# A hybrid decoder step: sampled tokens' PSUM tiles move into attention's five banks, and the filler projections get a second bank

## The chip, the cores and the metric

The kernel runs on one core of a Trainium2 chip. The metric is the device time of one execution in microseconds (us), as the median of several runs; less is better. Beside it stands a profile, which is one execution recorded instruction by instruction on the core's engines: PE (matrix products and transposes, written to PSUM), PEld (its weight loads), DVE (the vector engine), ACT (the activation engine), POOL and SP (which here mostly start transfers). PSUM has eight banks for all of them; each holds 128 x 512 float32 values.

## What is computed

One layer of a decoder for 1024 prompt tokens and 8 sampled tokens that share the weights. The prompt's and the samples' rows go through the same input projection, then two branches: sparse attention over the best 256 keys of each query, and a gated delta rule with a recurrent state. Both are gated, merged, and followed by a SwiGLU block.

```
xn = rms_norm(x, norm_mix)
h = xn @ w_in
q, k, v, iq, ik, iw, u, a, b, z, gl = jnp.split(h, pts, axis=-1)
...
o_a = attend(q, k, v, iq, ik, iw).reshape(B, T, BRANCH_WIDTH)
...
o_b, s_new = gated_delta_chunked(qb, kb, vb, g, beta, s0)
o_b = rms_norm(o_b.astype(x.dtype), delta_norm) * jax.nn.silu(z.reshape(B, T, H_B, DV_B))
...
proj = jnp.einsum('btnc,ncd->btnd', jnp.stack([o_a, o_b], axis=2), w_branch)
gates = jax.nn.sigmoid(gl.reshape(B, T, 2, D_MODEL))
x = x + jnp.sum(gates * proj, axis=2) @ w_out
x = x + (jax.nn.silu(gg) * uu) @ w_down
```

For the 8 sampled tokens, attend reads a paged cache of 1024 past keys (gathered by a page table) plus the token's own key, and the delta rule is one step on a given state of 8 x 4 matrices of 128 x 128.

## The kernel before

Float32 values are split into two parts (split, lines 185 to 188: ACT writes the high part, DVE subtracts to get the low part), and a product is made of three passes over them (mm3, lines 163 to 165). A projection of 128 output columns over all 1,032 tokens is done in three chunks of 344 tokens; each chunk fills one PSUM tile pj with 24 passes (12 for the merge), and is then emptied by ACT or DVE.

The stages that matter here come in this order in the program. `scan` runs the delta rule over eight chunks of the prompt, and projections of q, k, v and of gates (gate, L863 empties their tile into gs) between them. `attention` then does the following:

- For the eight blocks of 128 queries, from the longest (1,024 keys) to the shortest (128 keys), and two key groups each, `att_scores` makes the scores of four heads (L267 transposes the queries, L1024 and L1025 are the score products, L1026 on DVE adds the mask and takes the extreme of the row, L1031 on ACT takes the exponential, L1037 the reciprocal, L1039 on ACT and L1041 on DVE scale), and `att_out` transposes the weights (L1056), splits them (L187 into ph, L188 into pl) and multiplies with the values (L1060, L1061 into PV; L1066 and L1067 empty it). The scores of one group are woven with the output of the group ahead of it.
- The seven gates that are left (gate_steps) are woven with `sample_delta`, the delta step of the sampled tokens: L1458 to L1495 prepare it, L1482 multiplies the state, and eight times a mask (L1517, DVE, one buffer), a product (L1521, PE) and four updates (L1524, DVE) renew four matrices of the state, which are loaded and stored by SP (L1436, L1525).
- The first 21 chunks of `merge_b` (products of o with w_branch, emptied by L878) are woven with `sample_attend`, the attention of the sampled tokens: gathers of the cache by POOL (L1246), transposes (L1346), splits into kTp, products (L1358), a softmax, transposes of its weights (L1389) and products with the values (L1406).

The written order is only the input to a scheduler. It gives every engine one fixed queue of instructions, drawn from all stages whose buffers it has, and an engine then works through its queue in that order. Tiles of one tag in a pool share a ring of buffers (bufs) that is handed out in the order in which the program asks; a tile waits until the earlier holder of its buffer is done.

In `attention` eight banks are shared out like this: pj has one bank (the filler projections), tq has one (all tiles of sample_delta and sample_attend, through ptq), PT has five and PV has one (through pT and pv). `sample_attend` keeps its tiles in memory (the pools mergeg and sample) that the pool of `sample_delta` and the projections' input xhi, xlo give back.

Of the kernel before, what the change touches and what calls it, by code (L numbers as in the profile page):

```python
# [33 lines left out]
def weave(a, n, b=iter(()), m=0):  # L34

    x = 0
    for j, _ in enumerate(a):
        while x < m and x * n <= j * m:
            next(b, None)
            x += 1  # L40
    for _ in b:
        pass
# [12 lines left out]
class K:  # L55
# [849 lines left out]
    def attention(self, end_x):  # L905
        nc, I = self.nc, self.I
        ps, end_ps = self.pool("fillers", space=PSUM)
        self.pq = self.pf = ps
        self.pj_bufs = 1
        self.ps, end_pa = self.pool("att", space=PSUM)  # L910
        self.ap, end_a = self.pool("att")
        self.sd, end_sd = self.pool("sampled")
        last, last_n = iter(()), 0
        for i in ATT:
            for g in range(2):
                P = [None] * 4
                weave(self.att_scores(i, g, P), 13, last, last_n)
                last, last_n = self.att_out(i, g, P), i + 2
        weave(last, last_n)
        gates = list(self.gates)  # L920
        weave(self.gate_steps(gates), 5 * len(gates), self.sample_delta(), 13)
        end_x()
        end_sd()
        mg, end_mg = self.pool("mergeg")
        self.wk, self.end_sa = self.pool("sample", side="right")
        mp, end_m = self.pool("mergeb", side="right")
        steps = self.merge_b(self.load_split(mp, self.d_ob), mg)
        self.sample = self.sample_attend(mg)
        weave(islice(self.sample, 33), 25, islice(steps, BESIDE), BESIDE)
        end_pa()  # L930
        end_ps()
        self.pj_bufs, self.tp_bufs = 5, 2
        self.open_psum("ps5")
        self.pf, self.end_pf = self.pool("psm", space=PSUM)
        self.stage = self.sp.tile([128, 2048], F32, name="rs", tag="kvb", bufs=1)
        x0 = self.sp.tile([128, 4224], F32, name="x20", tag="S", bufs=1)
        self.x2h = [x0[:, 0:4 * T].rearrange("p (j t) -> p j t", j=4)]
        self.x_T(0)
        self.pq = self.ps
        for _ in steps:  # L940
            pass
        end_m()
        end_mg()
        end_a()
# [917 lines left out]
```

## Time and profile before

| | us |
|---|---|
| median of 3 runs (lowest to highest) | 1775.06 (1770.65 to 1778.87) |
| the profiled execution | 1773.84 |
| its span, first to last instruction | 1771.8 |
| PE busy | 1721.3 (97%) |
| PEld busy | 1662.9 (94%) |
| DVE busy | 1214.9 (69%) |
| ACT busy | 847.1 (48%) |
| POOL busy | 30.4 (2%) |

Busy time counts each moment once, however many instructions of an engine overlap in it. The mean duration in a group of instructions is longer than the step from one to the next where instructions are pipelined, so such durations must not simply be added on PE or DVE. The chain of work that ended last is 85% PE.

### The profile page before, as it was taken

Reading aid. Unit: us, or ns where it says so; the run is one execution under the profiler, and the core shown is the slowest. Engines: PE = TensorE matmul, PEld = TensorE weight load, DVE = VectorE, ACT = ScalarE, POOL = GpSimd, SP = SyncE. Lnnn points to the kernel's source line nnn. Section 1 sums busy time; section 2 is a strip of 40 time slices with the busy share of each in tenths; the row PEclk is TensorE's granted clock in tenths of the full one; section 3 lists DMA queues with packets and bytes.
Section 4 is the critical chain, followed back from the end, with each engine's and each line's share of the span. In section 5 each row is a group of like instructions: output and inputs, shape, how many; then the busy total and the mean of one; then the engine's idle time right before and its main releaser. Section 6 shows DMA issues by size and latency. Waiting matters only on the chain.

```text
span 1771.8 us, 31786 instructions
## 1 busy us (share of the span) xinstructions
PE 1721.3 (97%) x12300; PEld 1662.9 (94%) x12300; DVE 1214.9 (69%) x2809; ACT 847.1 (48%) x1575; POOL 30.4 (2%) x61
## 2 busy tenths in 40 slices
PE   6999999999999999999899999999999999999998
PEld 5998989999999989979898999999999999999998
DVE  7676658999799868799856488776666665733322
ACT  5566467777835436687534254443333333412112
POOL 0001100000000000000000000000000000000000
PEclk9999999999999999999999999999999999999999
DMA  6015434433645543354667444332222223722122
GB/s 209 30 38 159 127 101 137 147 97 114 175 127 160 174 144 95 111 166 144 220 203 237 141 128 138 102 108 85 72 85 84 79 78 128 236 68 81 45 81 69
DMA packets 293595, 218.02 MB, mean 123 GB/s; under 512 B 39292, under 2 KB 267456, under 8 KB 292412
## 3 DMA queue, kind: packets, MB, share of 16 engines
q1 hardware_dynamic: 291716, 205.50, 38.2%
q0 software_dynamic: 1728, 10.49, 1.7%
q8 instruction: 97, 1.59, 0.4%
q14 instruction: 54, 0.44, 0.1%
HBM read 154.17 MB, written 61.87 MB: 122 GB/s over the span
## 4 chain that ended last, share of the span: by engine, by line
PE 85%; DMA 6%; DVE 4%; ACT 3%; issue 2%; SPq 0%; POOL 0%; ACTq 0%; DVEq 0%; POOLq 0%
PE pj L163 15%; PE pj L165 15%; PE pj L164 15%; PE F L1734 2%; PE F L1736 2%; PE F L1735 2%; PE A L1734 2%; PE A L1735 2%; PE A L1736 2%; PE D L1734 2%; PE D L1736 2%; PE D L1735 2%; PE PT L1056 2%; PE B L1735 1%; PE B L1734 1%
## 5 line engine op out<-in xcount | busy, mean ns | idle before, releaser
L163 PE MATMUL pj<-xhi,whi 128*128 128x344 f32 x912 | 297.9, 327 | 5.2 <-ACT gs L863 4.3
L165 PE MATMUL pj<-xhi,wlo 128*128 128x344 f32 x912 | 293.7, 322 | 0.0
L164 PE MATMUL pj<-xlo,whi 128*128 128x344 f32 x912 | 292.9, 321 | 0.0
L187 ACT ACTIVATE whi<-wraw 128x1024 fp32r<-128x1024 f32 (+4 forms) x126 | 115.2, 914 | 245.4 <-PE pj L164 197.5
L163 PEld LDWEIGHTS pj<-xhi,whi 128*128 128x128 f32 x912 | 171.8, 188 | 9.5 <-ACT gs L863 5.6
L164 PEld LDWEIGHTS pj<-xlo,whi 128*128 128x128 f32 x912 | 171.7, 188 | 2.5 <-issue 1.1
L165 PEld LDWEIGHTS pj<-xhi,wlo 128*128 128x128 f32 x912 | 171.7, 188 | 1.2
L164 PE MATMUL pj<-act,whi 128*128 128x344 f32 x528 | 170.2, 322 | 0.0
L163 PE MATMUL pj<-act,whi 128*128 128x344 f32 x528 | 169.9, 322 | 0.0
L165 PE MATMUL pj<-act,wlo 128*128 128x344 f32 x528 | 168.8, 320 | 0.7 <-DVE wlo L188 0.7
L188 DVE TENSOR_TENSOR wlo<-wraw,whi 128x1024 fp32r<-128x1024 f32 (+3 forms) x104 | 116.4, 1119 | 48.2 <-ACT whi L187 47.3
L1798 DVE TENSOR_TENSOR x<-pj,x 128x344 f32<-128x344 f32 x96 | 48.7, 514 | 142.4 <-PE pj L165 142.4
L769 DVE TENSOR_SCALAR_CACHE_REDUCE kvb<-S,cand 128x384 bf16<-128x384 f32 (+3 forms) x128 | 103.7, 810 | 2.0
L165 PEld LDWEIGHTS pj<-act,wlo 128*128 128x128 f32 x528 | 99.3, 188 | 1.0 <-DVE wlo L188 1.0
L163 PEld LDWEIGHTS pj<-act,whi 128*128 128x128 f32 x528 | 99.3, 188 | 0.6
L164 PEld LDWEIGHTS pj<-act,whi 128*128 128x128 f32 x528 | 99.3, 188 | 0.0
L1735 PE MATMUL A<-hb,wlo 128*128 128x258 f32 x328 | 92.6, 283 | 0.0
L1734 PE MATMUL A<-hb,wlo 128*128 128x258 f32 x328 | 92.5, 282 | 0.0
L1736 PE MATMUL A<-hb,wlo 128*128 128x258 f32 x328 | 92.3, 282 | 0.0
L1734 PE MATMUL D<-hb,wx 128*128 128x258 f32 x308 | 87.1, 283 | 0.0
L1735 PE MATMUL D<-hb,wx 128*128 128x258 f32 x308 | 87.0, 282 | 0.0
L1736 PE MATMUL D<-hb,wx 128*128 128x258 f32 x308 | 87.0, 283 | 0.0
(604 smaller groups left out, 4785.8 us busy)
## 6 DMA issues: line engine op xcount, KB each, us to landing
wraw<-in_w_gate_up SPq DMA_DIRECT2D x50, 512.0 KB
wraw<-in_w_in SPq DMA_DIRECT2D x38, 512.0 KB
d_act<-x SPq DMA_DIRECT2D x41, 258.0 KB
araw<-d_act SPq DMA_DIRECT2D x20, 516.0 KB
d_g<-gs SPq DMA_DIRECT2D x48, 172.0 KB
wraw<-in_w_out SPq DMA_DIRECT2D x16, 512.0 KB
wraw<-in_w_branch SPq DMA_DIRECT2D x12, 512.0 KB
wraw<-in_w_down SPq DMA_DIRECT2D x16, 384.0 KB
```

The source lines that it names most:

```text
L163: nc.tensor.matmul(ps, lh, rh, start=(j == 0), stop=False)
L164: nc.tensor.matmul(ps, lh, rl, start=False, stop=False)
L165: nc.tensor.matmul(ps, ll, rh, start=False, stop=(j == last))
L187: self.nc.scalar.activation(hi, src, AF.Copy)
L188: self.nc.vector.tensor_tensor(lo, src, hi.bitcast(F32), op=ALU.subtract)
L769: nc.vector.tensor_scalar(junk[:r, :n], s, thr[:r, j:j + 1], 0.0, op0=ALU.is_lt, op1=ALU.add, accum_out=cnt[:r, j:j + 1])
L1056: nc.tensor.transpose(p[:, j, :], P[j][:, 128 * s:128 * s + 128], self.ident)
L1734: nc.tensor.matmul(p, lh, rh, start=(first and k == 0), stop=False, skip_group_check=True)
L1735: nc.tensor.matmul(p, lh, rl, start=False, stop=False, skip_group_check=True)
L1736: nc.tensor.matmul(p, ll, rh, start=False, stop=(k == 3), skip_group_check=True)
L1798: nc.vector.tensor_tensor(xv, p, xv, op=ALU.add)
```

## The change

The pool of the fillers gives both its banks to pj. The tiles of the sampled tokens (ptq) are for the time of `attention` taken from the ring PT, by setting ptq to pT; after the stage the original ptq is used again. All else is as written before, and nothing is added to or taken from the arithmetic. Line numbers after line 909 are one greater, and after line 932 two greater (L1521 becomes L1523).

```diff
--- before.py
+++ after.py
@@ -905,8 +905,9 @@
     def attention(self, end_x):
         nc, I = self.nc, self.I
         ps, end_ps = self.pool("fillers", space=PSUM)
-        self.pq = self.pf = ps
-        self.pj_bufs = 1
+        self.pf = ps
+        self.pj_bufs = 2
+        self.ptq = self.pT
         self.ps, end_pa = self.pool("att", space=PSUM)
         self.ap, end_a = self.pool("att")
         self.sd, end_sd = self.pool("sampled")
@@ -929,6 +930,7 @@
         weave(islice(self.sample, 33), 25, islice(steps, BESIDE), BESIDE)
         end_pa()
         end_ps()
+        del self.ptq
         self.pj_bufs, self.tp_bufs = 5, 2
         self.open_psum("ps5")
         self.pf, self.end_pf = self.pool("psm", space=PSUM)
```

The scheduler's queues change from the end of the scan on. Names in the rows below: pj is a projection's tile, PT a tile of the ring of five, tq the sampled tokens' tile before, PV attention's output; P are attention's weights, ph and pl their split parts; k2, q2 and v2 are keys, queries and values; sum, sk4, S0, st and skq belong to the sampled tokens' delta step; xhi, xlo, whi and wlo are a projection's operands.

On PE, in the middle of attention (the second largest block of queries), the queue before:

```order
L1060 MATMUL PV_7330<-ph_7357,v2_6586 128x512
L165 MATMUL pj_9237<-xhi_114,wlo_9205 128x344
L1061 MATMUL PV_7330<-pl_7358,v2_6586 128x512
L1024 MATMUL PT_7402<-k2_6585,q2_7311 128x448
L1025 MATMUL PT_7402<-k2_6585,q2_7311 128x448
L1521 MATMUL tq_9414<-sum_9412,sk4_9004 128x512
L1056 MATMUL PT_7407<-ident_84,P_7172 128x128
```

And the same place now:

```order
L1026 MATMUL PT_7398<-k2_6585,q2_7311 128x448
L1027 MATMUL PT_7398<-k2_6585,q2_7311 128x448
L1063 MATMUL PV_7330<-pl_7358,v2_6586 128x512
L1062 MATMUL PV_7330<-ph_7378,v2_6586 128x512
L1026 MATMUL PT_7402<-k2_6585,q2_7311 128x448
L1027 MATMUL PT_7402<-k2_6585,q2_7311 128x448
L1058 MATMUL PT_7407<-ident_84,P_7172 128x128
```

The projection pass (L165) and the sampled product (L1521) have left this place, and attention's own passes follow one another.

On PE, where the sampled tokens' delta step begins, the queue before, ahead of attention's first scores:

```order
L1458 MATMUL tq_8741<-ssq3_8643,ones_1543 128x96
L1459 MATMUL tq_8741<-sgd_8649,ones_1543 128x64
L267 MATMUL PT_6958<-ident_84,qn_6955 128x128 x2
L1482 MATMUL tq_8858<-skq_8640,st_8637 128x2 x8
L163 MATMUL pj_8972<-xhi_114,whi_8967 128x344
L164 MATMUL pj_8972<-xlo_115,whi_8967 128x344
L165 MATMUL pj_8972<-xhi_114,wlo_8968 128x344
```

And the place where it runs now, at the last two products of attention (L1062, L1063):

```order
L1062 MATMUL PV_8587<-ph_8593,v2_6586 128x512
L1484 MATMUL PT_8858<-skq_8640,st_8637 128x2 x2
L1063 MATMUL PV_8587<-pl_8594,v2_6586 128x512
L1484 MATMUL PT_8858<-skq_8640,st_8637 128x2 x4
L1484 MATMUL PT_8858<-skq_8640,S0_8891 128x2 x4
L1484 MATMUL PT_8858<-skq_8640,S0_8897 128x2 x4
L1495 MATMUL PT_9000<-sC_8744,ones_1543 128x32
L1496 MATMUL PT_9000<-ident_84,skr_8763 32x128
L1497 MATMUL PT_9000<-ident_84,skS_8764 32x128
L1523 MATMUL PT_9092<-sum_9034,sk4_9004 128x512
L1523 MATMUL PT_9192<-sum_9100,sk4_9004 128x512
```

The state products (L1482, now L1484) moved from attention's beginning to its end, and the eight products of L1523 stand in a row behind them, where projections stood between them before.

On DVE, the updates of the state before, among attention's splits (pl) and scores (L1026, ISA):

```order
L1517 TENSOR_TENSOR sum_9100<-sv4_9005,eye4_9006 128x512
L188 TENSOR_TENSOR wlo_9205<-wraw_9203,whi_9204 128x1024
L1026 ISA P_7172,st_7171<-PT_7173,msk_1966 128x448
L1026 ISA st_7171 128x1
L188 TENSOR_TENSOR pl_7152<-PT_7146,ph_7151 128x512
L1026 ISA P_7193,st_7171<-PT_7194,msk_1966 128x448
L1026 ISA st_7171 128x1
L188 TENSOR_TENSOR pl_7188<-PT_7182,ph_7187 128x512
L1026 ISA P_7172,st_7171<-PT_7177,msk_1966,st_7171 128x448
L1026 ISA st_7171 128x1
L1524 SCALAR_TENSOR_TENSOR st_8637<-st_8637,sC_8744,tq_9192 128x128 x4
L1517 TENSOR_TENSOR sum_9201<-sv4_9005,eye4_9006 128x512
```

And now, behind all of attention's work:

```order
L1526 SCALAR_TENSOR_TENSOR S0_9199<-S0_9199,sC_8744,PT_9293 128x128 x4
L1519 TENSOR_TENSOR sum_9302<-sv4_9005,eye4_9006 128x512
L1526 SCALAR_TENSOR_TENSOR S0_9300<-S0_9300,sC_8744,PT_9366 128x128 x4
L1519 TENSOR_TENSOR sum_9374<-sv4_9005,eye4_9006 128x512
L1526 SCALAR_TENSOR_TENSOR st_8637<-st_8637,sC_8744,PT_9404 128x128 x4
L1519 TENSOR_TENSOR sum_9412<-sv4_9005,eye4_9006 128x512
L1526 SCALAR_TENSOR_TENSOR st_8637<-st_8637,sC_8744,PT_9414 128x128 x4
L1519 TENSOR_TENSOR sum_9423<-sv4_9005,eye4_9006 128x512
L1526 SCALAR_TENSOR_TENSOR S0_9421<-S0_9421,sC_8744,PT_9425 128x128 x4
L1519 TENSOR_TENSOR sum_9434<-sv4_9005,eye4_9006 128x512
L1526 SCALAR_TENSOR_TENSOR S0_9432<-S0_9432,sC_8744,PT_9436 128x128 x4
```

The masks and updates alternate with nothing between them. Each mask uses the one buffer of the mask before.

## Rows read from the trace of the kernel before

**Rows 1.** the stretches table: busy us (x instructions) of PE, weight loads, DVE, ACT, POOL; granted clock, DMA share, GB/s:
```profile
580.00:646.00 66.00, 62.95 (x466) 58.93 (x465) 47.35 (x161) 24.39 (x58) 0.00 (x0) 1.00 0.50 145
646.00:872.00 226.00, 222.78 (x1425) 201.34 (x1426) 198.94 (x528) 161.02 (x335) 8.66 (x10) 1.00 0.46 145
872.00:912.00 40.00, 35.52 (x252) 30.75 (x251) 19.05 (x40) 9.68 (x20) 0.95 (x1) 0.91 0.53 183
```

**Rows 2.** the timeline of PE, first and last of 45 projection passes (start us, duration us):
```profile
870.32 0.32 PE L163 MATMUL pj<-o,whi 128*128 128x344 f32 x1
...
877.26 0.32 PE L165 MATMUL pj<-o,wlo 128*128 128x344 f32 x1
```

**Rows 3.** groups by line of PE, 646 to 872 us (busy us, mean ns, idle before):
```profile
L163 PE MATMUL pj<-xhi,whi 128*128 128x344 f32 x96 | 31.5, 328 | 0.0
...
L163 PE MATMUL pj<-o,whi 128*128 128x344 f32 x84 | 27.9, 332 | 0.0
...
L1521 PE MATMUL tq<-sum,sk 128*128 128x512 f32 x8 | 3.2, 394 | 0.0
```

**Rows 4.** the timeline of PE, sampled tokens' passes between attention's:
```profile
646.74 1.95 PE L1482 MATMUL tq<-skq,st 128*128 128x2 f32 x16
...
785.11 0.60 PE L1346 MATMUL tq<-ident,kvg 128*128 128x128 f32 x4
...
869.13 1.12 PE L1358 MATMUL tq<-kTp,q2S 128*128 128x256 f32 x8
```

**Rows 5.** groups by line of PE, 580 to 646 us:
```profile
L163 PE MATMUL pj<-xhi,whi 128*128 128x344 f32 x72 | 24.2, 336 | 2.4 <-ACT gs L863 2.4
```

**Rows 6.** groups by line of DVE, 646 to 872 us:
```profile
L188 DVE TENSOR_TENSOR pl<-PT,ph 128x512 fp32r<-128x512 f32 x72 | 48.9, 685 | 6.8 <-ACT ph L187 4.8 <-PE PV L1061 1.6
L1026 DVE CUSTOM_DVE_ANT_0 P<-PT,msk 128x512 f32<-128x512 f32 (+5 forms) x64 | 33.5, 534 | 3.2 <-PE PT L1025 2.8
L1026 DVE CUSTOM_DVE_ANT_0 P<-PT,msk,st 128x512 f32<-128x512 f32 (+3 forms) x32 | 20.6, 645 | 1.5 <-PE PT L1025 0.7
L1041 DVE TENSOR_SCALAR P<-P,st 128x1024 f32<-128x1024 f32 (+7 forms) x32 | 16.4, 517 | 0.5
L270 DVE TENSOR_TENSOR q<-PT,q 64x256 fp32r<-64x256 f32 x32 | 13.5, 422 | 2.5 <-ACT q L269 1.5
L1067 DVE TENSOR_TENSOR oT<-PV,pvt 64x512 f32<-64x512 f32 x16 | 11.0, 686 | 0.6 <-ACT pvt L1066 0.3
...
L1026 DVE DVE_READ_ACCUMULATOR2_ANT st<- 128x1 f32 x96 | 7.9, 82 | 0.0
...
L1517 DVE TENSOR_TENSOR sum<-sv,eye 128x512 fp32r<-128x512 f32 x8 | 5.5, 684 | 0.0
L1037 DVE RECIPROCAL st<-st 128x2 f32<-128x2 f32 x32 | 4.9, 157 | 1.0 <-ACT P L1031 0.8
```

**Rows 7.** the timeline of DVE, back to back:
```profile
684.41 0.61 DVE L1026 CUSTOM_DVE_ANT_0 P<-PT,msk 128x448 f32<-128x448 f32 x1
...
684.95 0.68 DVE L188 TENSOR_TENSOR pl<-PT,ph 128x512 fp32r<-128x512 f32 x1
685.55 0.67 DVE L1026 CUSTOM_DVE_ANT_0 P<-PT,msk,st 128x448 f32<-128x448 f32 x1
...
686.57 1.12 DVE L1524 SCALAR_TENSOR_TENSOR st<-st,sC,tq 128x128 f32<-128x128 f32 x4 [0.34 <-PE tq L1521]
```

**Rows 8.** groups by line of ACT, 646 to 872 us:
```profile
L1031 ACT ACTIVATE P<-P,st 128x1024 f32<-128x1024 f32 (+7 forms) x64 | 49.3, 771 | 18.1 <-DVE st L1026 17.8
L187 ACT ACTIVATE ph<-PT 128x512 fp32r<-128x512 f32 x72 | 41.8, 591 | 14.5 <-PE PT L1056 9.2 <-PE PV L1060 3.6 <-ACT gs L863 0.6
L1039 ACT ACTIVATE P<-P,st 128x1024 f32<-128x1024 f32 (+7 forms) x32 | 24.6, 772 | 1.8 <-DVE st L1037 1.6
```

**Rows 9.** the stretches table, around a fall of the granted clock:
```profile
880.00:885.00 5.00, 2.29 (x16) 1.46 (x15) 3.01 (x8) 0.58 (x2) 0.00 (x0) 0.86 0.78 270
885.00:890.00 5.00, 4.58 (x16) 4.58 (x17) 2.50 (x6) 1.79 (x4) 0.00 (x0) 0.50 0.68 188
```

## The prediction

> **What bounds the kernel now.** I read the stretches first, then the engines inside one of them. The change only acts between the end of the delta scan and the end of the sampled tokens' attention, so I cut that time in three [rows 1]: the scan's tail (580 to 646 us), prompt attention (646 to 872) and the sampled tail (872 to 912). In all three the tensor engine (PE) is the full engine: it is idle 66 - 62.95 = 3.05 us, 226 - 222.78 = 3.2 us and 40 - 35.52 = 4.5 us. VectorE (DVE) is busy 198.94 of the 226 us and ScalarE (ACT) 161.02. The reader should see how little can be won here: the PE idle time of all three stretches is 10.8 us, and that is the ceiling of any gain from shorter waits on PSUM. Everywhere else the program is not touched.
>
> Why is PE full during attention? Because four kinds of work are mixed there: attention's own matmuls, gate projections, merge projections, and the sampled tokens' products. A projection pass costs 0.158 us start to start: 44 steps from 870.32 to 877.26 [rows 2]. In the attention stretch 96 x 3 passes are gates and 84 x 3 are merges [rows 3], so 540 x 0.158 = 85 us are projections. The sampled products in it are 64 passes of L1482 at 1.95/16 = 0.12, 64 transposes at 0.60/4 = 0.15 and 64 products at 1.12/8 = 0.14 [rows 4], 26 us, less the drain of the last pass in each row; I take 22 us, and 4 us for the small ones. What is left of 222.8 us is attention itself: 222.8 - 85 - 26 = **112 us** of PE.
>
> **The change, part by part.** *A second bank for projections.* The wait that it takes away is on one row: L163 idle 2.4 us in the scan's tail behind ACT's evacuation gs [rows 5]. In the attention stretch the same row shows no idle time at all [rows 3], since PE had other work to run while ACT emptied the bank. So the direct gain is 2.4 us, and at most the 3.05 us above. The second bank has another effect: the scheduler can run gate projections back to back, and puts them earlier. Counted in the two orders, 2,448 passes on x stand on PE ahead of attention's first transposition before, and 2,633 now. These 185 passes x 0.158 = 29 us fall in the scan's tail, where PE has 3 us to spare, so attention starts about 26 us later, near 672 us. This by itself is no loss, as the same passes are then missing later: inside attention only 103 passes on x remain (288 before), and none of the merge's (240 before).
>
> *Sampled tiles in attention's banks.* These tiles are requested after all of attention's in the program, and a shared ring of five banks is handed out in that order. So sampled work that ran beside attention in its own bank (the eight products of L1521 stand among attention's rows before) now stands behind it: all eight products follow the last attention matmul on PE, and their 32 updates (L1524) and eight masks (L1517) stand in one block on DVE, with nothing in between. The merge's work follows as well, because its tiles lie in memory that the sampled state must leave first. SP's loads of the state and its stores move along with it. POOL's order is the same; its key gathers (L1246) now find free memory earlier, and cost nothing on the path.
>
> *What attention costs alone.* PE has 112 us of attention and 103 x 0.158 = 16 us of projections, together 128 us. DVE's attention work, by its rows [rows 6] 48.9 + 33.5 + 20.6 + 16.4 + 13.5 + 11.0 + 7.9 + 4.9 = 156.7 us, is a sum of durations that overlap: back to back a score of 448 columns, 0.61, and the reading of its minimum, 0.08, take 0.54 from start to start, and a split of 0.68 takes 0.60 (684.41 to 684.95 to 685.55) [rows 7]. At these steps the 156.7 us shrink to about 131 us. ACT's three largest groups alone are 49.3 + 41.8 + 24.6 = 116 us [rows 8]. So three engines have some 130 us each, and every tile passes through all three in turn, with two heads' groups in flight. Bounds for the stretch: 131 us if DVE never waits; 185 us if DVE is 70% full. I take **163 us**. About 17 us of it are the start, where 77 of the 103 passes stand between the first scores and DVE has only some 8 us of work; the other 131 - 8 = 123 us I take at 0.84 full (146 us). The nearest row is DVE's 198.94/226 = 0.88 [rows 1], and that was reached with much independent sampled work at hand, which is gone now, and the last heads are short and wait on each other. PE is then idle 163 - 128 = 35 us, from 672 to 835 us.
>
> *What the sampled tail costs alone.* Each of the eight state updates is a closed circle of one buffer: mask 0.68, product 0.39, four updates 1.12, and hand-overs of about 0.06 each [rows 3, 6, 7], some 2.25 us, so 18 us for eight, with 0.4 us of PE in each. Ahead of them stand the small vector operations and products of the state, some 4.5 us more. PE has about 8 us to do in these 22.5 us: 15 us idle. Then the attention of the sampled tokens begins with loads into memory that the state has just left (store, load, first transposes: some 5 us idle), and its eight halves run through ACT, DVE and PE in turn with only 24 projection passes between them (4 us idle); 3 us I keep for the softmax. Together **27 us**, with bounds of 15 (the state update half hidden behind the last heads) and 40 (every load late). After that merge projections fill PE as before.
>
> *Sum.* 35 + 27 = 62 us of new idle time, less the 10.8 us that PE idles there now, is 51 us. The profiled execution took 1773.84 us, so 1825 us. The median of the three runs, 1775.06, is 1.2 us above it, within their own spread (1770.65 to 1778.87), so I state **1825 us** against the median. About 0.5% (9 us) is what a measurement of this kernel can tell from no change.
>
> **The rivals.**
>
> *Tight packing, a smaller loss.* Attention runs near its floor (145 us, 17 us idle) and the state update overlaps the last heads (18 us): 17 + 18 - 11 = 24, so 1798 us. For it speaks that DVE fills 0.88 of the stretch while fighting for PE; against it that no covering work is left.
>
> *The clock falls.* After a stretch in which PE was busy 2.29 of 5 us, the granted clock was 0.50 (the 1.2 GHz level) for the next 5 us [rows 9]. If PE's gaps in attention and in the sampled tail bring the lower level for a quarter of the 163 us, PE's work there grows by a quarter of 128, 32 us; DVE's slack hides perhaps half, so I add 16 us there, 9 us in the tail and 5 us in the first merge passes: 30 us more, 1855 us. Against it: at 62.95 of 66 us the clock stayed 1.00, and the gaps may be short. The Trainium skill, TensorE: Matmul & The Clock Gate, section "A second HAM failure mode: psum-queue depth-cycling", describes such a case: cycling through PSUM banks leaves small gaps between groups of matmuls, and the clock swings. No run here shows it yet.
>
> *Faster: the banks were the limit.* The place is the five-bank ring. Sampled tiles were tied to one bank, and with five each transposition can run ahead of its split. If DVE holds attention to its floor of 131 us (3 us idle) and the sampled tail idles under 8 us because later projections can be drawn forward, then 3 + 2 - 11 = -6 to -8, some 1767 us. It decides at 10.8 us of new idle time in all: below that the change wins. Against it stand the orders: no projection is left to draw on in most of attention, and none stands between the eight state updates. The Trainium skill, Perfetto Trace Analysis, "Identifying Performance Opportunities", says that the same gap repeating on an engine that should be saturated can mean too little PSUM. Such gaps are scarce here, 3.2 us in 226 [rows 1], so by this trace the rule promises little.
>
> *Nothing happens.* The order on PE moves, but the moved work only changes places and PE stays full: 1775 us. It would need fillers in attention, which the order does not have.
>
> **How the numbers follow.** The forecast (roughly 1810 to 1845) gets 0.60, tight packing 0.17, the clock 0.14, faster 0.05, nothing 0.04. The low end takes in tight packing (1798); the high end takes DVE at 0.73 (57 us idle), the tail at its bound of 40, less 11: 86 us, some 1860, which also covers the clock case. So 1797 to 1862 us leaves out the last two cases and the tips of the others. Slower by over 0.5% has 0.60 + 0.17 + 0.14 = 0.91, within 0.5% 0.04, faster 0.05.
>
> **What would show it.** In the profile after, attention's first score should stand near 672 to 678 us and the last head end near 835; in between PE should be busy only about four fifths, with DVE above it, and L1056's successor and the score matmuls waiting for DVE and ACT. Behind it a stretch of some 25 us with PE mostly idle and the eight state updates on DVE in a row. The gs wait of L163 should be near zero. The sampled output products (L1406 before) should come some 50 us later. I am wrong if PE stays above 95% in attention, if the state updates' waits are filled by projections, or if the granted clock is at the lower level over tens of microseconds. Then the time is that of the rival named.

## The result, and the profile after

The changed kernel takes 1853.91 us (1853.48 to 1854.12, three runs) against 1775.06 us before: a ratio of 1.0441, 95% interval 1.0415 to 1.0466. It is slower, inside the range on record (1797 to 1862), 29 us above the forecast of 1825. The profiled execution has a span of 1852.2 us, 80.4 us more than before.

All of it lies between the end of the scan and the first half of the projection to w_out: the first product of the norm behind that half (L1632, now L1634) stands at 1101.3 us and stood at 1019.5, 81.8 us earlier. So the four stretches up to there hold the answer: the scan's tail, attention (first score to last product with the values), the sampled tokens' tail (to their last transposition, L1412, now L1414), and the merge with that first half of w_out. Stretches table of the changed kernel: length, then busy us (x instructions) of PE, weight loads, DVE, ACT, POOL, then granted clock, DMA share, GB/s:

```profile
580.00:678.00 98.00, 98.00 (x708) 95.44 (x707) 57.67 (x176) 34.52 (x78) 0.00 (x0) 1.00 0.48 142
678.00:843.00 165.00, 148.48 (x777) 115.69 (x775) 143.05 (x394) 132.71 (x283) 4.33 (x5) 0.93 0.19 59
843.00:976.00 133.00, 105.56 (x652) 89.84 (x652) 62.98 (x147) 25.33 (x46) 5.66 (x6) 0.81 0.55 174
976.00:1101.00 125.00, 114.25 (x822) 111.42 (x823) 71.60 (x137) 46.99 (x85) 0.00 (x0) 0.97 0.64 204
```

Against [rows 1]: PE, idle for 3.2 us of 226 in attention's old stretch, is now idle for 16.5 of 165, and for 27.4 of 133 behind it. In attention PE (148.48), DVE (143.05) and ACT (132.71) are all near the 165 us and none is full: they wait for each other. The clock column is new too: 0.93, 0.81, 0.97 where nearly all of it was 1.00.

Where each new microsecond of PE lies can be added up. In slices of about 4 us I took PE's idle time, its busy time x (1 - granted clock), and the rest, its busy time x granted clock. The middle one counts what the lower clock (1.2 in place of 2.4 GHz) cost PE if all its work then takes twice as long. A projection pass took 1.8 times as long there (0.287 us a step from 884.46 to 887.33 us, 0.158 in [rows 2]), so that column is rather too high and the last rather too low:

| 580 us to L1632, now L1634 | length | idle | lower clock | rest |
|---|---|---|---|---|
| before | 439.5 | 13.6 | 2.8 | 423.1 |
| after | 521.3 | 54.7 | 25.4 | 441.2 |
| difference | 81.8 | 41.1 | 22.6 | 18.1 |

The last two columns grow by 40.7 us, and the page of the profile has the same from its other end: PE's busy time, 1721.3 us before, is 40.1 us longer, though the work is the same. Its busy row and the shares of the chain that ended last:

```profile
PE 1761.4 (95%) x12300; PEld 1682.3 (91%) x12300; DVE 1218.3 (66%) x2809; ACT 847.4 (46%) x1575; POOL 30.8 (2%) x61
...
PE 83%; DMA 6%; DVE 6%; ACT 2%; issue 2%; SPq 0%; POOL 0%; ACTq 0%; DVEq 0%; POOLq 0%
```

The rest grows, as I read it, because products that come one by one cannot overlap with the next. The groups by line in attention show such products; how much of the 18.1 us they make up was not separated. The changed kernel, 678 to 843 us, then one line of the kernel before, 651 to 870 us (busy us, mean ns, idle before and who ended it):

```profile
L1058 PE MATMUL PT<-ident,P 128*128 128x128 f32 x288 | 46.0, 284 | 3.0 <-ACT P L1041 2.6 <-DVE st L1028 0.2
L1026 PE MATMUL PT<-k,q 128*128 128x512 f32 (+5 forms) x96 | 37.0, 388 | 3.6 <-DVE q L270 3.1
L1063 PE MATMUL PV<-pl,v 128*128 128x512 f32 x71 | 34.6, 488 | 7.5 <-DVE pl L188 7.4
L1062 PE MATMUL PV<-ph,v 128*128 128x512 f32 x72 | 31.7, 440 | 2.4 <-ACT ph L187 2.2
...
L163 PE MATMUL pj<-xhi,whi 128*128 128x344 f32 x26 | 8.4, 323 | 0.0
...
L1484 PE MATMUL PT<-skq,st 128*128 128x2 f32 x24 | 5.4, 342 | 0.0
L1484 PE MATMUL PT<-skq,S 128*128 128x2 f32 x16 | 3.6, 352 | 0.0
```

```profile
L1061 PE MATMUL PV<-pl,v 128*128 128x512 f32 x71 | 30.4, 429 | 1.1 <-DVE pl L188 1.0
```

PE now waits for DVE's splits (pl, 7.4 us), and 26 groups of three gate passes are all that covers it, where [rows 3] had 96 on gates and 84 on merges. The tail in slices of 5 us, from attention's last heads on:

```profile
815.00:820.00 5.00, 4.26 (x23) 2.78 (x22) 4.40 (x16) 4.77 (x14) 0.00 (x0) 1.00 0.12 30
820.00:825.00 5.00, 4.56 (x19) 3.51 (x19) 3.83 (x16) 3.85 (x13) 0.00 (x0) 0.60 0.12 28
...
835.00:840.00 5.00, 5.00 (x26) 5.00 (x26) 3.27 (x16) 0.60 (x1) 0.00 (x0) 0.50 0.35 100
...
860.00:865.00 5.00, 1.53 (x2) 0.57 (x2) 3.46 (x11) 0.00 (x0) 0.00 (x0) 0.50 0.67 175
...
875.00:880.00 5.00, 0.00 (x0) 0.00 (x0) 1.47 (x5) 1.55 (x4) 0.00 (x0) 0.50 0.72 197
...
885.00:890.00 5.00, 5.00 (x28) 4.62 (x28) 1.70 (x4) 1.33 (x3) 0.00 (x0) 0.50 0.40 72
890.00:895.00 5.00, 5.00 (x26) 3.76 (x26) 2.62 (x5) 2.21 (x5) 0.94 (x1) 0.73 0.33 66
```

From 820 to 890 us PE runs at or near the lower level, first through the short heads, then through the state. The timeline of PE there (start, duration, in brackets the idle time before it and what ended it):

```profile
862.71 0.76 PE L1523 MATMUL PT<-sum,sk 128*128 128x512 f32 x1 [1.91 <-DVE sum L1519]
865.29 0.80 PE L1523 MATMUL PT<-sum,sk 128*128 128x512 f32 x1 [1.82 <-DVE sum L1519]
...
873.35 0.76 PE L1523 MATMUL PT<-sum,sk 128*128 128x512 f32 x1 [1.91 <-DVE sum L1519]
880.37 0.56 PE L1315 MATMUL PT<-ident,sP 8*128 8x8 f32 x4 [6.26 <-DMA sP<-d_q]
```

One state update takes 2.66 us ((873.35 - 862.71) / 4), its product 0.76 us in place of 394 ns [rows 3], and then the load of the sampled queries (sP) holds PE for 6.26 us more. The chain of the profile shows what that load waited for (start, duration):

```profile
871.23 4.26 DMA ldr<-d_ob
...
878.14 2.09 DMA sP<-d_q
```

The load itself takes 2.09 us. It stands in SP's queue behind loads of the merge's operand (ldr, which has two buffers): SP could issue the third of those only when DVE had split the first (L188, done at 876.7 us), then issued a fourth, and sP at 877.7. So the order of SP's queue is part of these 6.26 us, and not only the memory of the state.

### The profile page after: what moved, and what is told of

Same layout as the page of the kernel before. It is cut to its first block, busy times and chain, and to the rows that moved or that the text cites. A ratio compares the mean times of both kernels' runs of the same rounds, so it can differ in the third digit from the quotient of the medians.

```text
span 1852.2 us, 31827 instructions
## 1 busy us (share of the span) xinstructions
PE 1761.4 (95%) x12300; PEld 1682.3 (91%) x12300; DVE 1218.3 (66%) x2809; ACT 847.4 (46%) x1575; POOL 30.8 (2%) x61
## 4 chain that ended last, share of the span: by engine, by line
PE 83%; DMA 6%; DVE 6%; ACT 2%; issue 2%; SPq 0%; POOL 0%; ACTq 0%; DVEq 0%; POOLq 0%
PE pj L163 15%; PE pj L165 15%; PE pj L164 15%; PE F L1736 2%; PE F L1737 2%; PE F L1738 2%; PE A L1736 2%; PE A L1737 2%; PE A L1738 2%; PE D L1736 2%; PE D L1738 2%; PE D L1737 2%; PE B L1737 1%; PE B L1736 1%; PE B L1738 1%
## 5 line engine op out<-in xcount | busy, mean ns | idle before, releaser
L163 PE MATMUL pj<-xhi,whi 128*128 128x344 f32 x912 | 297.4, 326 | 3.7 <-ACT gs L863 1.8
L165 PE MATMUL pj<-xhi,wlo 128*128 128x344 f32 x912 | 294.9, 323 | 0.0
L163 PEld LDWEIGHTS pj<-xhi,whi 128*128 128x128 f32 x912 | 172.7, 189 | 6.8 <-ACT gs L863 2.4
L165 PEld LDWEIGHTS pj<-xhi,wlo 128*128 128x128 f32 x912 | 172.6, 189 | 1.1
L163 PE MATMUL pj<-act,whi 128*128 128x344 f32 x528 | 169.8, 322 | 0.0
L165 PE MATMUL pj<-act,wlo 128*128 128x344 f32 x528 | 168.8, 320 | 0.7 <-DVE wlo L188 0.7
L188 DVE TENSOR_TENSOR wlo<-wraw,whi 128x1024 fp32r<-128x1024 f32 (+3 forms) x104 | 116.5, 1120 | 56.1 <-ACT whi L187 55.0
L165 PEld LDWEIGHTS pj<-act,wlo 128*128 128x128 f32 x528 | 99.3, 188 | 1.0 <-DVE wlo L188 1.0
L163 PEld LDWEIGHTS pj<-act,whi 128*128 128x128 f32 x528 | 99.3, 188 | 0.6
```

Of the source, the lines that this page charges most:

```text
L163: nc.tensor.matmul(ps, lh, rh, start=(j == 0), stop=False)
L165: nc.tensor.matmul(ps, ll, rh, start=False, stop=(j == last))
L188: self.nc.vector.tensor_tensor(lo, src, hi.bitcast(F32), op=ALU.subtract)
```

## The experiments

My theory: a ring of banks is handed out in the order of requests, so the sampled work, requested behind all of attention, runs behind it, the merge follows, and PE loses its cover. Rivals: the second projection bank does the harm by drawing the gates ahead; the lower clock carries the loss; the sharing itself costs, whatever the order. Each ratio is against the kernel before, on the same chip.

### Which of the two edits

*The ring alone*: one projection bank, sampled tiles in attention's ring.

```diff
-        self.pj_bufs = 2
+        self.pj_bufs = 1
         self.ptq = self.pT
```

> Sampled tiles in attention's ring, but projections keep one bank. On PE's queue 264 gate passes now stand inside attention (77 in the changed kernel), still no merge pass and no state update. Theory (the ring's order takes the sampled work and the merges out of attention): most of the loss stays; the 187 passes that are back (x 0.158 us = 29 us) fill idle time of PE in attention, so about 1854 - 25 = 1828 us (1815 to 1840). Rival (the second bank draws the gates forward and that is the loss): back to 1775 us (within 10). Rival (the granted clock, not the idle time, is the loss): PE is busier in attention, the clock stays up there, about 1810 us.

Measured: 1859.67 us, ratio 1.0487 (1.0425 to 1.0548), not to be told apart from the changed kernel. The ring by itself makes the whole loss. What I expected of it, 1828, missed: attention did begin at 650 again, but ended only 7 us earlier.

```profile
650.00:836.00 186.00, 171.28 (x965) 143.73 (x965) 146.41 (x396) 139.53 (x293) 3.61 (x5) 0.95 0.22 67
836.00:972.00 136.00, 102.42 (x636) 86.31 (x637) 63.57 (x148) 24.12 (x44) 5.66 (x6) 0.84 0.50 160
972.00:1103.00 131.00, 118.56 (x846) 115.60 (x845) 71.62 (x137) 47.79 (x87) 0.00 (x0) 0.95 0.64 205
```

The 187 gate passes that stay inside (x965 for x777 instructions of PE) make attention 186 us long where it was 165: they are not free there. And the 7 us are lost again behind it (136 and 131 us in place of 133 and 125).

*The second bank alone*, with a ring of four, since there are eight banks; and beside it *the ring of four alone* (the second of these two edits without the first), both from the kernel before:

```diff
-        self.pj_bufs = 1
+        self.pj_bufs = 2
...
-        return self.ps.tile([128, 4, 128], F32, name="PT", tag="PT", bufs=5)
+        return self.ps.tile([128, 4, 128], F32, name="PT", tag="PT", bufs=4)
```

> The second bank alone: projections have two banks, sampled tiles keep their own, and the ring gives up one bank (four). PE's queue has 155 gate passes, 252 merge passes, all state updates and sampled scores inside attention. Theory (the ring's order is the loss): 1775 us, within 12; at most the 2.4 us of the gs wait gained, some lost to the ring of four. Rival (the second bank is the loss): 1830 to 1855 us.

> Control for the bank-only run: the kernel before with a ring of four banks, nothing else. Both theories: 1770 to 1790 us. What it differs from the kernel before is the price of the fifth bank; what the bank-only run differs from it is the price or gain of the second projection bank (theory: within 6 us; rival: 50 us or more).

Measured: 1810.39 us (1.0209, 1.0149 to 1.0269) and 1790.47 us (1.0093, 1.0067 to 1.0120). The fifth bank is worth some 17 us, and the second projection bank costs 20 us on top, where I expected no more than a few: neither my 1775 us nor the rival's 1830 to 1855 came. So the bank is no help even with the sampled tiles apart. PE's idle time over the whole stretch rises from 19.3 to 29.2 us, 6.4 us of this in attention, where 155 gate passes stand in place of 279: the gates that ran ahead are missing there. Only with the ring shared does that loss vanish in the greater one.

*The sampled tiles in the projections' two banks*, attention's ring for itself:

```diff
-        self.ptq = self.pT
+        self.ptq = lambda: ps.tile([128, 4, 128], F32, name="pj", tag="pj", bufs=2)
```

> Sampled tiles share the projections' two banks, in place of attention's ring. They are requested in turn with the projections, so PE's queue has 363 gate passes, 180 merge passes, the eight state updates and 40 of 64 sampled scores inside attention. Theory (what decides is behind whom a tile is requested in its ring): 1775 us, within 12, since the cover is back. Rival (a sampled tile without a bank of its own is late, whoever it shares with): 1820 us or more.

Measured: 1808.62 us (1.0178, 1.0115 to 1.0240). Attention has its ring for itself, and 45 us of the changed kernel's 79 come back; I expected the whole, and the rival 1820 us or more. By the landmarks attention is 11 us longer than before (230 for 219) and the sampled tail 25 (68 for 42), while the last stretch has its old 107 us again. PE stands idle even in the scan's tail:

```profile
630.00:635.00 5.00, 0.66 (x4) 0.42 (x4) 2.13 (x6) 1.77 (x5) 0.00 (x0) 1.00 0.49 135
635.00:640.00 5.00, 1.09 (x4) 0.72 (x4) 3.31 (x14) 1.49 (x2) 0.00 (x0) 0.57 0.01 2
```

So sharing two banks with the projections costs too; how much of it is order and how much sharing, this run does not tell.

### The tail's pieces

*Products that nobody reads*, to keep PE's clock up: two behind each output step of the last four blocks, one with each load of the state, three behind each group of updates, six at the end.

```diff
+            if i <= 3:
+                for _ in range(2):
+                    nc.tensor.matmul(p.rearrange("p a b -> p (a b)"), self.v2[:, s, g, :], ph, start=True, stop=True)
...
+                    nc.tensor.matmul(p[:, 128:512], self.ident, flat(S0)[:, 0:384], start=True, stop=True)
...
+                for _ in range(3):
+                    nc.tensor.matmul(flat(p), k4, self.k2[:, 0, 0, 0:512], start=True, stop=True)
+        for _ in range(6):
+            nc.tensor.matmul(flat(p), self.ident, flat(S0), start=True, stop=True)
```

> The changed kernel with PE products added that nobody reads: two of 512 columns behind each output step of the last four blocks of queries, one of 384 columns (float32) with each load of the state, three of 512 columns behind each group of state updates and six of 512 columns (float32) at the end. All else keeps its place in PE's queue. If the clock carries the part of the loss that my forecast did not have (29 us): the granted clock stays near 1.00 from 820 to 890 us instead of 0.50 to 0.6, and the time falls to 1832 us (1822 to 1842). Rival (the tail is set by DVE's circle and by loads, and PE's clock there is without effect): 1854, or up to 10 us more for the added products.

Measured: 1848.23 us (1.0413, 1.0381 to 1.0444), 6 us less than the changed kernel by the medians, with intervals that overlap. The added products held the clock in attention, but not in the state updates:

```profile
677.00:836.00 159.00, 146.78 (x820) 115.35 (x818) 142.88 (x394) 132.42 (x283) 4.32 (x5) 1.00 0.20 61
836.00:971.00 135.00, 115.66 (x699) 95.53 (x698) 62.65 (x147) 25.29 (x46) 5.64 (x6) 0.87 0.54 171
...
865.00:870.00 5.00, 3.19 (x7) 2.09 (x8) 3.29 (x10) 0.95 (x2) 0.00 (x0) 0.50 0.71 191
...
875.00:880.00 5.00, 5.00 (x15) 2.38 (x13) 1.33 (x3) 1.72 (x4) 0.00 (x0) 0.99 0.40 96
```

Attention is 6 us shorter (159 for 165) at a clock of 1.00 in place of 0.93. The tail, where the clock stayed at 0.50 until the last six products, is no shorter. So at most some 6 us of the clock's 25 are seen to come back, and the intervals don't exclude none. For the tail the run decides nothing: the clock was not held there, and the added products themselves stretched a state update from 2.66 to 3.29 us (L1527 at 850.59, 853.88 and 857.17 us).

*Two buffers for the mask* (sum, from one to two):

```diff
-                um = wk.tile([128, 4, 128], F32R, name="sum", tag="sum", bufs=1)
+                um = wk.tile([128, 4, 128], F32R, name="sum", tag="sum", bufs=2)
```

> The changed kernel with two buffers for the mask of the state update instead of one, so that the next mask need not wait for the product. The circle of mask, product and four updates (2.25 us by my sum, 2.7 as measured at the lower clock) opens to DVE's own 1.7 us: eight times 0.8 to 1.0. If the tail lies one to one on the path, 1847 us (1845 to 1850); if something else (loads, the merge's transfers) ends later, 1854.

Measured: 1849.94 us (1.0428, 1.0394 to 1.0462), 4 us less by the medians, inside the range of the first expectation, but again with overlapping intervals.

```profile
862.31 0.76 PE L1523 MATMUL PT<-sum,sk 128*128 128x512 f32 x1 [0.97 <-DVE srqk L200]
864.13 0.77 PE L1523 MATMUL PT<-sum,sk 128*128 128x512 f32 x1 [1.05 <-DVE srt L198]
874.12 0.56 PE L1315 MATMUL PT<-ident,sP 8*128 8x8 f32 x4 [9.22 <-DMA sP<-d_q]
```

The circle opened to 1.7 to 1.8 us, and the last product is 9.2 us earlier (864.13 for 873.35). 1.8 us of that the first product had already (852.69 for 854.49), so the eight updates won 7.4. But PE then waits 9.22 us for the load in place of 6.26. The chain now runs through the state's own transfers: a store (3.02 us), the load of the next state into its buffer (2.32 us) and, behind the last updates, the store of the sampled output (2.41 us), all ahead of the load of the queries. Of 9 us some 6 arrive at that load, and of these 4 or so at the end.

### Order of requests, or sharing

*The delta step requested among attention's groups*, one step behind each group, banks as in the changed kernel; then *all sampled work among the groups*, three requests at a time.

```diff
+        delta = self.sample_delta()
         for i in ATT:
             for g in range(2):
                 P = [None] * 4
                 weave(self.att_scores(i, g, P), 13, last, last_n)
                 last, last_n = self.att_out(i, g, P), i + 2
+                next(delta, None)
...
-        weave(self.gate_steps(gates), 5 * len(gates), self.sample_delta(), 13)
+        weave(self.gate_steps(gates), 5 * len(gates), delta, 13)
```

and in the second, after each of the last eleven groups,

```diff
+                if x == 6:
+                    weave(self.gate_steps(gates), 5 * len(gates), delta, 13)
...
+                if x >= 6:
+                    weave(islice(self.sample, 3), 3, islice(steps, 2), 2)
```

> The changed kernel, but the thirteen steps of the sampled tokens' delta step are requested one by one among attention's sixteen groups, not behind them; the sampled tokens' attention is still requested behind. Same banks, same arithmetic. In the queue 157 merge passes now stand inside attention (0 in the changed kernel). Theory (a ring is handed out in the order of requests, so what is requested behind attention runs behind it): the eight state products run inside attention, the bare tail of some 35 us behind the last head is gone, half of the merge passes cover attention again; 1800 us (1785 to 1815). Rival (sharing five banks is what costs, wherever the tiles are requested): above 1835.

> The changed kernel, but the delta step is requested among the first six of attention's groups, and the sampled tokens' attention and the merge's first chunks among the other ten. 264 merge passes and all 64 score products of the sampled tokens then stand inside attention in PE's queue, as in the kernel before (240 and 64). Theory of request order: nearly all of the loss comes back; what remains is the cost of the second projection bank, which was 20 us with a ring of four; 1785 us (1770 to 1800). Rival (sharing five banks costs in itself): above 1820.

Measured: 1833.66 us (1.0329, 1.0306 to 1.0352) and 1831.09 us (1.0317, 1.0294 to 1.0341). The order counts, since 20 and 23 us come back, but the theory missed both times: with the second, every sampled score product and 264 merge passes stood inside attention (240 before the change), and still it was 46 us above the theory. There the rival's figure came true (above 1820).

Two suspects were left in it, the second bank and the sharing. *One projection bank, all woven*, and *the same with the bank left over in the ring* (six):

```diff
-        self.pj_bufs = 2
+        self.pj_bufs = 1
...
-        return self.ps.tile([128, 4, 128], F32, name="PT", tag="PT", bufs=5)
+        return self.ps.tile([128, 4, 128], F32, name="PT", tag="PT", bufs=6)
```

> The kernel in which all sampled work is requested among attention's groups, with one projection bank instead of two; the sampled tokens' tiles stay in attention's ring of five (seven of the eight banks are used). In PE's queue 264 gate passes, 264 merge passes and all 64 score products of the sampled tokens then stand inside attention (before 279, 240 and 64). Theory (two causes, each taking cover away from attention: the second bank draws the gates ahead of it, the ring pushes what is requested later behind it): both are undone, 1780 us (1765 to 1795). Rival (sampled tiles in attention's ring cost in themselves, because a slow load holds the whole ring up): about 1830, as with two projection banks.

> The same, with the bank left over given to the ring (six banks in it). From four to five banks the ring was worth some 17 us; theory: a sixth is worth 0 to 10 us more, 1772 us (1758 to 1790), about the kernel before. Rival (order or a slow load holds the ring up, more banks don't help): as with five, within 4 us.

Measured: 1820.41 us (1.0255, 1.0238 to 1.0272) and 1809.53 us (1.0198, 1.0181 to 1.0215). The second bank costs 11 us in this order, a sixth bank in the ring wins 11 (0 to 10 expected), and the theory of order alone has fallen: 46 us stay with a ring of five and 35 with six, with the cover of the kernel before back in attention. Both were expected at 1772 to 1780; the rival's 1830 was nearer for the first.

*The same order with the banks of before* is the control, one bank for the sampled tokens and five for attention:

```diff
-        self.pf = ps
+        self.pq = self.pf = ps
         self.pj_bufs = 1
-        self.ptq = self.pT
```

And *a finer weave in the shared ring*: drip draws one sampled request behind every fourth step of the scores (every is 4; the definition of drip is left out here).

```diff
-                weave(self.att_scores(i, g, P), 13, last, last_n)
+                weave(drip(self.att_scores(i, g, P), src, every), 13, last, last_n)
...
-                    weave(islice(self.sample, 3), 3, islice(steps, 2), 2)
```

> The kernel before with all sampled work requested among attention's groups, as in the kernel with one projection bank, but with the banks of before: one for the sampled tokens, five for attention, one for projections. PE's queue then holds 279 gate passes, 228 merge passes and 64 sampled score products inside attention, almost as before (279, 240, 64). If the sampled tiles in attention's ring are what cost 45 us there: 1775 us (1768 to 1785). If it was my new order of requests: about 1820.

> One projection bank and a shared ring of five, as in the woven kernel that took 1820 us, but the sampled requests are spread evenly, one behind every fourth step of attention's scores, where that kernel requested three at a time between two groups. Theory A (three sampled tiles in a row hold up the ring; spread out they don't): 1790 us (1780 to 1802). Theory B (each sampled tile that waits for its own chain holds up all later tiles of the ring, however the requests are spread): 1820 us (1810 to 1830).

Measured: 1774.33 us (0.9989, 0.9972 to 1.0005) and 1801.40 us (1.0138, 1.0119 to 1.0157). The control is the kernel before to within its error, so my order of requests costs nothing by itself. It differs from the 1820 us kernel only in the bank of the sampled tiles: that one bank is worth 46 us. The control uses eight banks, though, and the 1820 us kernel seven; against the kernel with six banks in the shared ring, which also uses eight, the separate bank is worth 35 us (1809.53 to 1774.33). The finer weave ends at the upper edge of theory A's range: spreading the requests, three to each group as before, won 19 of the 46 us. The other 27 stay with this spread, which is what theory B is about, though its 1820 us did not come.

The stretches from the first score to the last product with the values, first the control, then the finer weave:

```profile
655.00:873.00 218.00, 213.66 (x1366) 192.84 (x1365) 191.02 (x507) 158.60 (x330) 9.21 (x10) 1.00 0.44 138
```

```profile
657.00:920.00 263.00, 252.49 (x1557) 223.00 (x1556) 200.87 (x538) 163.04 (x333) 9.67 (x11) 0.94 0.40 128
```

In the finer weave the sampled output products are among the x1557, so the stretch holds more work. Up to the first product of the norm the finer weave is 33.6 us longer, 12.8 of them idle, 15.1 the lower clock, 5.7 the rest; its profiled execution (1807.32 us) was the longest of its four, hence more than the 27 us of the medians. Two places stand out. PE's longest wait is the sampled softmax in the middle of its queue (waited for, us in total, times, longest):

```profile
PE PT L1409 <- DVE sP L1401: 6.7, 1, 6.7
```

The control waits 1.6 us at the same transposition. And the state products fall together into runs, in which the clock falls to 0.50 (below). Which part of the 27 us each of these carries was not separated.

No version beat the kernel before.

## Why the prediction was right, and where not

**Scan's tail: right.** 185 passes were to move ahead of attention and put the first score at 672 to 678 us; it stands at 678.2. L163 waits 0.0 us for gs there (2.4 in [rows 5]).

**Sampled work behind attention: right**, but the mechanism named is less than half of the loss. With one projection bank, where the loss is 85 us, the order of requests costs 39 us (1859.67 to 1820.41, the first known to some 11 us) and requesting three in a row 19 more (to 1801.40). The last 27 us (to the control's 1774.33) are not in my working at all: I took the sharing of a ring to matter only through its order.

**Attention alone, 163 us: right in length (165.0), wrong in make-up.** I had PE at 128 us of work and 35 idle. It was busy 148.5 and idle 16.5. 10 us of that is the lower clock, and 138.5 - 128 = 10.5 us are left. Some 4.5 of them are 40 state products (L1484, 5.4 + 3.6 us at a clock of 0.50) that ran between the last heads and that I had put into the tail. The other 6 I read as products without neighbours to overlap with: L1063 has a mean of 488 ns (486 from 780 to 815 us, where the clock was 1.00) where it had 429 in attention before. I took PE's share as a remainder out of a full stretch, where every pass hid the next one's start. The row of the weight loads would have warned: 115.7 of 165 us now, 201.34 of 226 in [rows 1]. The Trainium skill, Perfetto Trace Analysis, "Identifying the Most-Contended Engine", says that the share of time in which PE's row shows products is no good measure of how near it is to its limit, and that the busy share of the weight loads is; this trace agrees, 0.90 for the one and 0.70 for the other in attention now.

**Sampled tail, 27 us idle: right as a sum (27.4), by errors that cancel.** The eight updates took 2.7 us each, not 2.25, and the state products and small steps 11.3 us behind the last head (843.2 to 854.5), not 4.5: 18.9 us idle up to 875 us, where I had 15. The load holds PE for 6.3, not 5, and SP's queue has a part in it, which my working did not have. The sampled attention then idles for some 3 us, not 7.

**"After that merge projections fill PE as before": wrong.** Before, passes on oa (the merge of the attention branch) covered the sampled output products. Now the 288 passes on o (the delta branch), 240 of which had run in attention, have to do it, and the others run later. Behind the last sampled transposition stand 96 groups of three passes on oa, 78 before: 18 x 3 x 0.158 = 8.5 us of passes that came too late to cover anything there. The groups by line show what PE waits for in the last stretch, before (912 to 1020 us) and now (976 to 1101 us):

```profile
L163 PE MATMUL pj<-oa,whi 128*128 128x344 f32 x77 | 24.9, 323 | 0.0
```

```profile
L163 PE MATMUL pj<-oa,whi 128*128 128x344 f32 x96 | 32.5, 350 | 7.3 <-DVE gt L898 4.9 <-ACT oa L187 2.4
```

The stretch's idle time went from 2.8 to 10.8 us. My sum had nothing for it. No run tests this stretch by itself.

**The clock: the term that I left out of the sum.** I gave it as a rival with 0.14, as if it were another case than the forecast, and priced it at 30 us (16 in attention, 9 in the tail, 5 in the first merge passes). It came together with the forecast, at 10.0, 12.6 and 2.8 us. A forecast with 15 us of idle PE in a row was not consistent with a clock of 1.00, and [rows 9] had said so. By the sign of being wrong that I had put on record, the lower level over tens of microseconds, this part was wrong: the clock was 0.50 from 835 to 890 us. That its price and the miss are alike (1855 and 1853.9) proves less than it seems, since PE's idle time came out 10 us lower than forecast (41.1 for 51), the rest 18.1 higher, and holding the clock in attention gave back only 6 us.

**Sum.** In place of 51 + 0 + 0 the trace has 41.1 (idle) + 22.6 (clock) + 18.1 (the rest, as I read it no overlap) = 81.8. That the range held it is in part luck. Its upper end stood for DVE at 0.73 full and a tail of 40 us idle; DVE was at 0.87 (143.05 of 165) and the tail idled for 27.4. Two small slips change nothing: DVE at 70% full is 131 / 0.7 = 187 us, not 185, and the faster rival put 2 us of idle tail into its sum where its condition says under 8.

**The second bank: wrong.** I had a gain of 2.4 us, and the moved gates as "no loss" by themselves. It lost 20 us with a ring of four and 11 with all woven. In the changed kernel it makes no difference that the runs can tell.

**Faster, tight packing, nothing: none came.** The faster rival's rule, that a repeating gap can mean too little PSUM (the Trainium skill, Perfetto Trace Analysis, "Identifying Performance Opportunities"), agrees with the ring's own runs: the fifth bank was worth 17 us (PE's idle time over the whole stretch is 19.3 us with four and 13.6 with five) and the sixth, in the shared ring, 11. Here the banks came with a second user, and that cost more.

## What to carry to other kernels

A buffer ring is also a queue, handed out in the order of requests: give it to one kind of work. Here one bank of its own for the slow work was worth 46 us, and the same bank as a sixth in the shared ring only 11. That a holder which waits for its own chain stops the others is the likely reason for what order and spreading did not bring back, but no run shows it by itself. Before a change takes covering work away, count the cover that is left in each stretch, and price a bare PE stretch with the lower clock and without overlap, not by idle time alone. And a projection that is ready early is not a gain if it was the filler of a later stretch.

## What the runs showed of the hardware

PE's clock fell while its row showed it busy throughout. In the finer weave, slices of 5 us:

```profile
660.00:665.00 5.00, 5.00 (x31) 4.58 (x30) 3.77 (x13) 3.70 (x7) 0.00 (x0) 1.00 0.00 0
665.00:670.00 5.00, 5.00 (x36) 5.00 (x36) 3.56 (x16) 3.02 (x4) 0.00 (x0) 0.74 0.47 138
670.00:675.00 5.00, 5.00 (x25) 5.00 (x24) 1.74 (x8) 1.21 (x3) 0.00 (x0) 0.50 0.67 212
```

What ran from 664.98 on was 32 state products of two columns, one after another, then 16 more (three projection passes and a transposition lie between):

```profile
664.98 1.84 PE L1502 MATMUL PT<-skq,st 128*128 128x2 f32 x16
666.68 2.91 PE L1502 MATMUL PT<-skq,S 128*128 128x2 f32 x16
...
670.78 3.41 PE L1502 MATMUL PT<-skq,st 128*128 128x2 f32 x16
```

The fall lies among the second sixteen, which took 2.91 us where the first took 1.84. Projection passes behind them went at 0.29 us a step until 684 us. In the kernel before the same 64 products start between 646.7 and 659.4 us among scores and projection passes, and the clock there is 1.00 throughout. But the first sixteen stand in a row there too, and in the control, which has the same sixteen in a row, the clock did fall at their end, for some 3 us:

```profile
649.31 2.24 PE L1489 MATMUL tq<-skq,st 128*128 128x2 f32 x16
...
652.13 0.49 PE L165 MATMUL pj<-xhi,wlo 128*128 128x344 f32 x1
```

So a full row on PE is no assurance of its clock; why it fell in the control and not in the kernel before, the runs do not settle. The Trainium skill, TensorE: Matmul & The Clock Gate, section "A second HAM failure mode: psum-queue depth-cycling", puts a swinging clock down to small gaps between groups of products that cycle through PSUM banks; attention's last heads agree (0.60 in 820 to 825 us, behind 4.26 of 5 us busy), while this fall had no gap that the rows show.
